# Scores of a forgetting attention: three float32r products of two-part queries and keys in place of one float32 product

## The chip, the cores and the metric

The kernel runs on one core of one Trainium2 chip. The metric is the device time of one execution in microseconds (us); a kernel is run several times and the median is given. The engines are named as the profile names them: PE is the TensorE matmul, PEld its weight load, DVE is VectorE, ACT is ScalarE, POOL is GpSimd, SP is the queue that issues the weight transfers.

## The reference

A decoder trunk of two layers over 256 tokens of width 2048, all in float32. Layer 0 has a dilated attention beside a convolution module, layer 1 has the "second mixer", a forgetting attention of 16 heads of 128 dimensions; each layer ends with a gated feed-forward part of width 5632. The change touches the scores of the second mixer alone:

```
u = h @ w_in
q, k, v, fl = jnp.split(u, [dC, 2 * dC, 3 * dC], axis=-1)
q = q.reshape(B, S, N_HEADS_C, HEAD_DIM) * (HEAD_DIM ** -0.5)
logf = jax.nn.log_sigmoid((fl + b_f).astype(F32))
...
Fc = jnp.cumsum(logf, axis=1)
...
s = jnp.einsum("bqhe,bkhe->bhqk", qi, k, preferred_element_type=F32)
s = s + (Fi[..., :, None] - Ft[..., None, :])
s = jnp.where(ti[:, None] >= pos[None, :], s, -jnp.inf)
p = jax.nn.softmax(s, axis=-1)
```

## The kernel before

Every large product is made in float32r, a rounded form of float32, with each operand split in two parts, hi (the value rounded to float32r) and lo (what is left). The normed tokens stand in `xs` as hi and lo side by side. Weights come from memory as `raw` (1 MB transfers on the SP queue), and `stream` splits each piece: ACT writes `whi` (L95), DVE writes `wlo` (L96), with four buffers of each.

`panel_b` makes 512 output columns, transposed, in four accumulators: per 128 x 128 weight tile one product of 512 columns, hi weight by both token parts (L109), and one of 256 columns, lo weight by the hi tokens (L110). `panel_a` does the same with the tokens as the stationary operand: three products of 512 columns (L122 to L124). `whole` adds the two halves of an accumulator (ACT L116, DVE L118).

The second mixer works through four groups of four heads. For each group there is a panel of queries (`qk1`, `acc_q`, 128 + 128 products), a panel of keys (`acc_k`), then the scores, then a panel of values (`acc_v`). `qk1` ends with one multiplication of all four heads by the norm factor (L527, DVE, 128 x 1024). The first group also makes the forget gates, whose cumulative sums go by small transfers into `fq` and `fk`, tiles of only 4 rows (partitions).

`softmax_t` makes the scores of four heads, called m = 0 to 3. A head has two blocks of queries: the first looks at 128 keys, the second at 256. Each block is one float32 product of q and k (L225; 128 rows, 128 or 256 columns) and, accumulated on it, one float32r product of `fq` and `fk` (L227; 4 rows, the same columns), which adds the forget bias. DVE then adds the mask and takes the maximum (L229), ACT makes the exponentials (L235), and so on. In layer 0 the same function runs without the bias, so there the float32 products stand alone (tile `s_e`; in layer 1 `s_o`).

The order on each engine is set by a scheduler when the program is built; it puts the scores of a group into the stream of the value panel's products, three heads together and the fourth some 16 products later. Each engine works in its own order and waits only for data and for free buffers.

Of the kernel before, what the change touches and what calls it, by code (L numbers as in the profile page):

```python
# [9 lines left out]
F32 = mybir.dt.float32  # L10
F32R = mybir.dt.float32r
I32 = mybir.dt.int32
AF = mybir.ActivationFunctionType
ALU = mybir.AluOpType
AX = mybir.AxisListType

P = 128
T = 256
# [23 lines left out]
def trunk(ctx, tc, a):  # L42
    nc = tc.nc
    V, S, PE, G = nc.vector, nc.scalar, nc.tensor, nc.gpsimd
# [8 lines left out]
    def misc(name):  # L53
        return pms.tile([P, 512], F32, tag="misc", name=name)
# [58 lines left out]
    def whole(out, acc, name):  # L113

        half = wk.tile([P, T], F32, tag="half", name=f"half_{name}", bufs=3)
        S.copy(half, acc[:, T:])  # L116
        out = half if out is None else out
        V.tensor_tensor(out=out, in0=acc[:, :T], in1=half, op=ALU.add)  # L118
        return out
# [17 lines left out]
    def cols(w, panel, k0=0):  # L137

        def part(c, n):
            kt = k0 // P + c  # L140
            return w[panel, kt // 4, :, kt % 4:kt % 4 + n, :]
        return part
# [31 lines left out]
    def rstd_from(parts, n, name):  # L174

        ps = misc(f"ss_{name}")
        for t in range(2):
            for i, ssq in enumerate(parts):
                PE.matmul(ps[:, t:t + 1], ssq[:, t * P:(t + 1) * P], ones[:, 0:1], start=i == 0, stop=i == len(parts) - 1)
        r = rsqrt_cols(ps[:, 0:2], 1.0 / n, name)  # L180
        return r, along_free(r, name)
# [32 lines left out]

    ROWS = ((0, 0, P), (1, P, T))

    def softmax_t(pool, qf, kf, mask, name, bias=None, act_scale=False):
        nm = wk.tile([P, 8], F32, tag="nm", name=f"nm_{name}")
        den = wk.tile([P, 8], F32, tag="den", name=f"den_{name}")
        ps = [pool.tile([P, 384], F32, tag="pt", name=f"pt_{name}{m}", bufs=8) for m in range(4)]  # L220
        for m, p in enumerate(ps):
            s = misc(f"s_{name}{m}")
            for t, c0, nk in ROWS:
                o = s[:, c0:c0 + nk]
                PE.matmul(o, qf[:, m, t * P:(t + 1) * P], kf[:, m, 0:nk], start=True, stop=bias is None)  # L225
                if bias is not None:
                    PE.matmul(o, bias[0][:, m, t * P:(t + 1) * P], bias[1][:, m, 0:nk], start=False, stop=True)  # L227
            for t, c0, nk in ROWS:
                V.tensor_tensor_reduce(out=p[:, c0:c0 + nk], in0=s[:, c0:c0 + nk], in1=mask[:, c0:c0 + nk], scale=1.0,  # L229
                                       scalar=-3.0e38, op0=ALU.add, op1=ALU.max, accum_out=nm[:, 2 * m + t:2 * m + t + 1])  # L230
        V.tensor_scalar(out=nm, in0=nm, scalar1=-1.0, scalar2=None, op0=ALU.mult)
        for m, p in enumerate(ps):
            for t, c0, nk in ROWS:
                i = 2 * m + t
                S.activation(p[:, c0:c0 + nk], p[:, c0:c0 + nk], AF.Exp, bias=nm[:, i:i + 1], accum_out=den[:, i:i + 1])  # L235
        V.reciprocal(out=den, in_=den)
        for m, p in enumerate(ps):
            for t, c0, nk in ROWS:
                w = den[:, 2 * m + t:2 * m + t + 1]
                if act_scale:  # L240
                    S.activation(p[:, c0:c0 + nk], p[:, c0:c0 + nk], AF.Copy, scale=w)
                else:
                    V.tensor_scalar(out=p[:, c0:c0 + nk], in0=p[:, c0:c0 + nk], scalar1=w, scalar2=None, op0=ALU.mult)
            tp = misc(f"tp_{name}{m}")
            for b in range(3):
                PE.transpose(tp[:, b * P:(b + 1) * P], p[:, b * P:(b + 1) * P], ident)
            S.copy(p, tp[:, :384])
        return ps
# [12 lines left out]
    with ExitStack() as ph:  # L261
        mx = ph.enter_context(tc.tile_pool(name="mx0", bufs=1))
# [139 lines left out]
        qf = [qk_panel(512 * hg, rq, f"q{hg}") for hg in range(2)]  # L402
        pts = []
        pace[0] = P_K
        for hg in range(2):
            kf = qk_panel(1024 + 512 * hg, rb, f"k{hg}")
# [102 lines left out]
    with ExitStack() as ph:  # L509
        mx = ph.enter_context(tc.tile_pool(name="mx1", bufs=1))  # L510
        w_in, w_out = a["od_w_in"], a["od_w_out"]
        mask = mx.tile([P, 384], F32, name="mask1")
        G.dma_start(out=mask, in_=a["c_mask"][:, 384:768])
        bf = mx.tile([P, 1], F32, name="bf")
        G.memset(bf[96:P, :], 0.0)
        G.dma_start(out=bf[P - NHC:P, :], in_=a["od_b_f"].rearrange("l h -> h l"))
        y2 = mx.tile([P, KT, 2, T], F32R, name="y21")
        rcol, rb = rstd_from([ssq1], D, "m1")
        rq = mx.tile([P, T], F32, name="rq")
        V.tensor_scalar(out=rq, in0=rb, scalar1=SC, scalar2=None, op0=ALU.mult)  # L520

        def qk1(c0, r, name):
            acc = panel_b(cols(w_in, c0 // 512), x2, list(range(KT)), name)
            full = mx.tile([P, 4, T], F32, tag=name[0] + "1", name=name, bufs=2)
            for m in range(4):
                whole(full[:, m, :], acc[m], f"{name}{m}")
            V.tensor_tensor(out=full, in0=full, in1=r.unsqueeze(1).broadcast_to([P, 4, T]), op=ALU.mult)  # L527
            return full

        def forget_gates():  # L530

            acc = panel_b(lambda c, n: a["od_w_f"], x2, list(range(KT)), "fl", order=(0,))
            g0 = slice(96, P)
            z = mx.tile([P, T], F32, name="z")
            e = mx.tile([P, T], F32, name="e")
            fc = mx.tile([P, T], F32, name="fc")
            whole(z, acc[0], "fl")
            V.tensor_tensor(out=z[g0, :], in0=z[g0, :], in1=rb[g0, :], op=ALU.mult)
            V.tensor_scalar(out=z[g0, :], in0=z[g0, :], scalar1=bf[g0, :], scalar2=None, op0=ALU.add)
            V.scalar_tensor_tensor(out=e[g0, :], in0=z[g0, :], scalar=-1.0, in1=z[g0, :], op0=ALU.mult, op1=ALU.min)  # L540
            S.activation(e[g0, :], e[g0, :], AF.Exp)
            S.activation(e[g0, :], e[g0, :], AF.Ln, bias=1.0)
            V.scalar_tensor_tensor(out=z[g0, :], in0=z[g0, :], scalar=0.0, in1=e[g0, :], op0=ALU.min, op1=ALU.subtract)
            V.tensor_tensor_scan(out=fc[g0, :], data0=ones[g0, 0:1].broadcast_to([32, T]), data1=z[g0, :], initial=0.0,
                                 op0=ALU.mult, op1=ALU.add)

            fhl = mx.tile([P, 4, T], F32R, name="fhl")
            fv = fhl.bitcast(F32)
            V.tensor_copy(fhl[g0, 0, :], fc[g0, :])
            V.tensor_tensor(out=fhl[g0, 1, :], in0=fc[g0, :], in1=fv[g0, 0, :], op=ALU.subtract)  # L550
            V.tensor_scalar(out=fhl[g0, 2:4, :], in0=fv[g0, 0:2, :], scalar1=-1.0, scalar2=None, op0=ALU.mult)
            return fv

        for hg in range(4):
            qf = qk1(512 * hg, rq, f"q1{hg}")
            if hg == 0:
                fv = forget_gates()
            fq = mx.tile([4, 4, T], F32R, tag="fq", name=f"fq{hg}")
            fk = mx.tile([4, 4, T], F32R, tag="fk", name=f"fk{hg}")
            G.memset(fq.bitcast(F32), 1.0)  # L560
            G.memset(fk.bitcast(F32), 1.0)
            f0 = P - NHC + 4 * hg
            for r in range(2):
                G.dma_start(out=fq.bitcast(F32)[r:r + 1, :, :], in_=fv[f0:f0 + 4, r, :])
                G.dma_start(out=fk.bitcast(F32)[2 + r:3 + r, :, :], in_=fv[f0:f0 + 4, 2 + r, :])
            kf = qk1(2048 + 512 * hg, rb, f"k1{hg}")
            pts = softmax_t(mx, qf, kf, mask, f"o{hg}", bias=(fq, fk))
            va = panel_a(cols(w_in, 8 + hg), x2, list(range(KT)), f"v1{hg}")
            vt = mx.tile([P, 2, 512], F32, tag="vt1", name=f"vt1{hg}")
            for t in range(2):  # L570
                S.activation(vt[:, t, :], va[t], AF.Copy, scale=rcol[:, t:t + 1])
            for m in range(4):
                weigh_v(pts[m], vt, m, y2, 4 * hg + m, f"o{hg}{m}")

        ssq2 = new_ssq("f1")
        for i in range(4):
            acc = panel_b(cols(w_out, i), lambda k: y2[:, k, :, :], list(range(KT)), f"oc{i}")
            add_x(acc, i, then=lambda kt: finish_x(kt, 48 + kt, ssq2, "f1"))
# [3 lines left out]
    o = fin.tile([P, 2, D], F32, name="o")  # L582
# [141 lines left out]
```

## Time and profile before

| | us |
|---|---|
| median of 3 runs | 2268.2 |
| lowest and highest of them | 2265.68, 2268.28 |
| the profiled execution's own time | 2266.76 |
| its span, first to last instruction | 2265.0 |
| PE busy | 2226.5 (98%) |
| DVE busy | 1510.7 (67%) |
| ACT busy | 1131.3 (50%) |

The second mixer lies at about 1117 to 1510 us of the span. In the profile a matmul's duration runs from its issue to its modelled end and includes the passage through the array, so neighbours overlap: what a product costs is read from the distance to the next one's start. The records mark all matmul operands as f32, whether float32 or float32r. One float32 product written in the code stands in the trace as two weight loads and two matmuls.

### The profile page before, as it was taken

Reading aid. Unit: us, or ns where it says so; the run is one execution under the profiler, and the core shown is the slowest. Engines: PE = TensorE matmul, PEld = TensorE weight load, DVE = VectorE, ACT = ScalarE, POOL = GpSimd, SP = SyncE. Lnnn points to the kernel's source line nnn. Section 1 sums busy time; section 2 is a strip of 40 time slices with the busy share of each in tenths; the row PEclk is TensorE's granted clock in tenths of the full one; section 3 lists DMA queues with packets and bytes.
Section 4 is the critical chain, followed back from the end, with each engine's and each line's share of the span. In section 5 each row is a group of like instructions: output and inputs, shape, how many; then the busy total and the mean of one; then the engine's idle time right before and its main releaser. Section 6 shows DMA issues by size and latency. Waiting matters only on the chain.

```text
span 2265.0 us, 30815 instructions
## 1 busy us (share of the span) xinstructions
PE 2226.5 (98%) x12142; PEld 1915.6 (85%) x12142; DVE 1510.7 (67%) x2307; ACT 1131.3 (50%) x1619; POOL 45.5 (2%) x77
## 2 busy tenths in 40 slices
PE   8999889999999999999999999999999999999997
PEld 7888778888888888888888888888888888888886
DVE  6999988776754576666655555666766644676644
ACT  6667655454443344444554444555444433444433
POOL 2000000000000000000010000000000000000001
PEclk9999899999999999999999999999999999999999
DMA  7554345555555545555545444555455555545453
GB/s 254 186 183 171 129 151 186 186 186 187 186 186 194 189 176 204 185 187 186 190 151 186 166 152 165 186 186 203 177 191 192 187 187 194 193 172 203 168 190 126
DMA packets 60225, 411.90 MB, mean 182 GB/s; under 512 B 7232, under 2 KB 7936, under 8 KB 11696
## 3 DMA queue, kind: packets, MB, share of 16 engines
q1 hardware_dynamic: 59328, 408.62, 50.7%
q8 instruction: 95, 1.56, 0.3%
q10 hardware_dynamic: 144, 1.05, 0.1%
q14 instruction: 50, 0.41, 0.1%
q0 software_dynamic: 608, 0.26, 0.0%
HBM read 407.75 MB, written 2.10 MB: 181 GB/s over the span
## 4 chain that ended last, share of the span: by engine, by line
PE 97%; DVE 1%; ACT 1%; DMA 0%; issue 0%; SPq 0%; ACTq 0%; DVEq 0%
PE acc_g L109 15%; PE acc_u L109 14%; PE acc_g L110 7%; PE acc_u L110 7%; PE acc_d L109 7%; PE acc_q L109 4%; PE acc_k L109 4%; PE acc_d L110 4%; PE acc_oc L109 3%; PE acc_ag L109 2%; PE acc_q L110 2%; PE acc_k L110 2%; PE acc_v L122 2%; PE acc_v L123 2%; PE acc_d L122 2%; PE acc_d L124 2%
## 5 line engine op out<-in xcount | busy, mean ns | idle before, releaser
L109 PE MATMUL acc_g<-xs,whi_g 128*128 128x512 f32 x1408 | 493.1, 397 | 0.0
L109 PE MATMUL acc_u<-xs,whi_u 128*128 128x512 f32 x1408 | 481.9, 395 | 0.0
L110 PE MATMUL acc_g<-xs,wlo_g 128*128 128x256 f32 x1408 | 388.8, 280 | 0.0
L110 PE MATMUL acc_u<-xs,wlo_u 128*128 128x256 f32 x1408 | 370.0, 279 | 0.0
L96 DVE TENSOR_TENSOR wlo_g<-raw_g,whi_g 128x1024 fp32r<-128x1024 f32 x176 | 215.1, 1223 | 166.2 <-ACT whi_g L95 166.2
L109 PEld LDWEIGHTS acc_g<-xs,whi_g 128*128 128x128 f32 x1408 | 262.6, 188 | 60.7
L95 ACT CAST whi_u<-raw_u 128x1024 fp32r<-128x1024 f32 x176 | 185.1, 1052 | 239.9 <-PE acc_u L109 122.0
L109 PEld LDWEIGHTS acc_u<-xs,whi_u 128*128 128x128 f32 x1408 | 260.1, 188 | 52.7
L96 DVE TENSOR_TENSOR wlo_u<-raw_u,whi_u 128x1024 fp32r<-128x1024 f32 x176 | 213.1, 1221 | 116.6 <-ACT whi_u L95 116.6
L95 ACT CAST whi_g<-raw_g 128x1024 fp32r<-128x1024 f32 x176 | 184.9, 1051 | 198.1 <-PE acc_u L109 91.3
L96 DVE TENSOR_TENSOR wlo_d<-raw_d,whi_d 128x1024 fp32r<-128x1024 f32 x136 | 166.5, 1224 | 161.5 <-ACT whi_d L95 161.3
L110 PEld LDWEIGHTS acc_u<-xs,wlo_u 128*128 128x128 f32 x1408 | 265.0, 188 | 9.0
L110 PEld LDWEIGHTS acc_g<-xs,wlo_g 128*128 128x128 f32 x1408 | 265.6, 189 | 3.0 <-DVE wlo_g L96 0.2
L95 ACT CAST whi_d<-raw_d 128x1024 fp32r<-128x1024 f32 x136 | 143.0, 1051 | 207.2 <-PE acc_d L109 118.9
L109 PE MATMUL acc_d<-hp,whi_d 128*128 128x512 f32 x704 | 245.2, 394 | 0.0
L110 PE MATMUL acc_d<-hp,wlo_d 128*128 128x256 f32 x704 | 194.4, 283 | 0.0
L109 PEld LDWEIGHTS acc_d<-hp,whi_d 128*128 128x128 f32 x704 | 131.3, 188 | 28.8
L110 PEld LDWEIGHTS acc_d<-hp,wlo_d 128*128 128x128 f32 x704 | 132.3, 188 | 1.9
L109 PE MATMUL acc_q<-xs,whi_q 128*128 128x512 f32 x384 | 133.8, 396 | 0.0
L109 PE MATMUL acc_k<-xs,whi_k 128*128 128x512 f32 x384 | 131.7, 394 | 0.0
L110 PE MATMUL acc_q<-xs,wlo_q 128*128 128x256 f32 x384 | 104.5, 282 | 0.0
L110 PE MATMUL acc_k<-xs,wlo_k 128*128 128x256 f32 x384 | 102.0, 279 | 0.0
(296 smaller groups left out, 3858.4 us busy)
## 6 DMA issues: line engine op xcount, KB each, us to landing
raw_g<-in_ffn_w_up SPq DMA_DIRECT2D x88, 1024.0 KB, 4.8
raw_u<-in_ffn_w_up SPq DMA_DIRECT2D x88, 1024.0 KB, 4.8
raw_d<-in_ffn_w_down SPq DMA_DIRECT2D x68, 1024.0 KB, 4.8
raw_q<-in_od_w_in SPq DMA_DIRECT2D x16, 1024.0 KB, 4.8
raw_k<-in_od_w_in SPq DMA_DIRECT2D x16, 1024.0 KB, 4.8
raw_v<-in_od_w_in SPq DMA_DIRECT2D x16, 1024.0 KB, 4.8
raw_oc<-in_od_w_out SPq DMA_DIRECT2D x16, 1024.0 KB, 4.8
raw_e<-in_ffn_w_down SPq DMA_DIRECT2D x16, 1024.0 KB, 4.7
```

The source lines that it names most:

```text
L95: S.copy(hi, rv[:, h:h + half, :])
L96: last = V.tensor_tensor(out=lo, in0=rv[:, h:h + half, :], in1=hi.bitcast(F32), op=ALU.subtract)
L109: PE.matmul(acc[m], hi[:, j, ms], x.rearrange("p a t -> p (a t)"), start=k == 0, stop=False)
L110: PE.matmul(acc[m][:, :T], lo[:, j, ms], x[:, 0, :], start=False, stop=k == len(kts) - 1)
L122: PE.matmul(o, xh, hi, start=first, stop=False)
L123: PE.matmul(o, xh, lo, start=False, stop=False)
L124: PE.matmul(o, xl, hi, start=False, stop=last)
```

## The change

`qk1` no longer hands out the float32 queries and keys: a new function `split4` makes a hi part (ACT, a copy to float32r) and a lo part (DVE, a subtraction), each 128 x 1024, into tiles `sq` and `sk`. Each float32 product of a score becomes three float32r products of the same size: hi by hi, hi by lo, lo by hi. The bias product stays as the last of the group. The tile `full` now has one buffer shared by queries and keys; `sq` and `sk` have one each. Layer 0 keeps its float32 products.

```
+    def split4(pool, full, tag, name):
+
+        two = pool.tile([P, 2, 4, T], F32R, tag=tag, name=name, bufs=1)
+        S.copy(two[:, 0], full)
+        V.tensor_tensor(out=two[:, 1], in0=full, in1=two.bitcast(F32)[:, 0], op=ALU.subtract)
+        return two
...
-                o = s[:, c0:c0 + nk]
-                PE.matmul(o, qf[:, m, t * P:(t + 1) * P], kf[:, m, 0:nk], start=True, stop=bias is None)
-                if bias is not None:
-                    PE.matmul(o, bias[0][:, m, t * P:(t + 1) * P], bias[1][:, m, 0:nk], start=False, stop=True)
+                o, ts = s[:, c0:c0 + nk], slice(t * P, (t + 1) * P)
+                if bias is None:
+                    PE.matmul(o, qf[:, m, ts], kf[:, m, 0:nk], start=True, stop=True)
+                else:
+                    PE.matmul(o, qf[:, 0, m, ts], kf[:, 0, m, 0:nk], start=True, stop=False)
+                    PE.matmul(o, qf[:, 0, m, ts], kf[:, 1, m, 0:nk], start=False, stop=False)
+                    PE.matmul(o, qf[:, 1, m, ts], kf[:, 0, m, 0:nk], start=False, stop=False)
+                    PE.matmul(o, bias[0][:, m, ts], bias[1][:, m, 0:nk], start=False, stop=True)
...
-            full = mx.tile([P, 4, T], F32, tag=name[0] + "1", name=name, bufs=2)
+            full = mx.tile([P, 4, T], F32, tag="qk1", name=name, bufs=1)
...
-            return full
+            return split4(mx, full, name[0] + "2", f"s{name}")
```

On PE, in the value panel of the first head group, the scores stood like this (s_o00 and s_o01 are the scores of heads m = 0 and 1, acc_v10 a value accumulator; the first 128x128 and 128x256 of a head are its two blocks):

```order
L122 MATMUL acc_v10_0_10475<-whi_v10_6_10529,xs_78 128x512
L225 MATMUL s_o00_10409<-k10_10389,q10_10135 128x128
L227 MATMUL s_o00_10409<-fk0_10210,fq0_10209 128x128
L225 MATMUL s_o00_10409<-k10_10389,q10_10135 128x256
L227 MATMUL s_o00_10409<-fk0_10210,fq0_10209 128x256
L225 MATMUL s_o01_10416<-k10_10389,q10_10135 128x128
L227 MATMUL s_o01_10416<-fk0_10210,fq0_10209 128x128
```

Now the same place reads:

```order
L124 MATMUL acc_v10_0_10497<-whi_v10_6_10551,xs_78 128x512
L235 MATMUL s_o00_10415<-sk10_10406,sq10_10149 128x128
L235 MATMUL s_o01_10426<-sk10_10406,sq10_10149 128x128
L235 MATMUL s_o02_10437<-sk10_10406,sq10_10149 128x128
L122 MATMUL acc_v10_1_10498<-whi_v10_6_10551,xs_78 128x512
L123 MATMUL acc_v10_1_10498<-wlo_v10_6_10552,xs_78 128x512
L124 MATMUL acc_v10_1_10498<-whi_v10_6_10551,xs_78 128x512
L236 MATMUL s_o00_10415<-sk10_10406,sq10_10149 128x128
L237 MATMUL s_o00_10415<-sk10_10406,sq10_10149 128x128
L238 MATMUL s_o00_10415<-fk0_10213,fq0_10212 128x128
L235 MATMUL s_o00_10415<-sk10_10406,sq10_10149 128x256
L236 MATMUL s_o00_10415<-sk10_10406,sq10_10149 128x256
```

The scores begin five value products later, the first hi-by-hi products of three heads stand ahead of the rest, and every bias product still stands alone between products of 128 rows. The other three groups and the fourth head of each group change in the same way.

On ACT and DVE one instruction each is added per panel of queries and per panel of keys. On DVE, behind the key panel of the first group, before:

```order
L118 TENSOR_TENSOR k_10389<-acc_k_3_10220,half_k_10399 128x256
L527 TENSOR_TENSOR k_10389<-k_10389,rb_m_9959 128x1024
L96 TENSOR_TENSOR wlo_v_8_10548<-raw_v_8_10545,whi_v_8_10547 128x1024
L96 TENSOR_TENSOR wlo_v_10_10564<-raw_v_8_10545,whi_v_10_10563 128x1024
L229 ISA pt_o_10405,nm_o_10403<-s_o_10409,mask_9935 128x128
```

and now:

```order
L118 TENSOR_TENSOR k_10392<-acc_k_3_10220,half_k_10402 128x256
L538 TENSOR_TENSOR k_10392<-k_10392,rb_m_9959 128x1024
L221 TENSOR_TENSOR sk_10406<-k_10392,sk_10406 128x1024
L96 TENSOR_TENSOR wlo_v_8_10570<-raw_v_8_10567,whi_v_8_10569 128x1024
L96 TENSOR_TENSOR wlo_v_10_10586<-raw_v_8_10567,whi_v_10_10585 128x1024
L96 TENSOR_TENSOR wlo_v_12_10604<-raw_v_12_10601,whi_v_12_10603 128x1024
L240 ISA pt_o_10411,nm_o_10409<-s_o_10415,mask_9935 128x128
```

The split of the keys stands ahead of the next weight split (`wlo_v_8`), and the split `wlo_v_12` has moved ahead of the first maximum. On ACT the copy `sk<-k` stands ahead of `whi_v_8` in the same way, behind the last `half_k`. Nothing else moves on any engine, and POOL and SP issue what they did, in the same order.

## Rows read from the trace of the kernel before

**Rows 1.** The page's first part: busy us, share and instructions per engine.
```profile
PE 2226.5 (98%) x12142; PEld 1915.6 (85%) x12142; DVE 1510.7 (67%) x2307; ACT 1131.3 (50%) x1619; POOL 45.5 (2%) x77
```

**Rows 2.** Windows of the second mixer: busy us per engine, PE clock.
```profile
1160.00:1180.00 20.00, 20.00 (x85) 15.05 (x84) 10.17 (x25) 5.95 (x6) 2.62 (x4) 1.00 0.42 152
```

**Rows 3.** Timeline of PE, scores of the first group: start us, duration us, instruction.
```profile
1166.12 0.39 PE L122 MATMUL acc_v<-whi_v,xs 128*128 128x512 f32 x1
1166.35 0.38 PE L225 MATMUL s_o<-k,q 128*128 128x128 f32 x2
1166.66 0.32 PE L227 MATMUL s_o<-fk,fq 4*128 4x128 f32 x1
...
1167.86 0.49 PE L225 MATMUL s_o<-k,q 128*128 128x128 f32 x2
1168.27 0.32 PE L227 MATMUL s_o<-fk,fq 4*128 4x128 f32 x1
1168.53 0.70 PE L225 MATMUL s_o<-k,q 128*128 128x256 f32 x2
1169.16 0.38 PE L227 MATMUL s_o<-fk,fq 4*128 4x256 f32 x1
1169.47 0.49 PE L225 MATMUL s_o<-k,q 128*128 128x128 f32 x2
...
1170.77 0.38 PE L227 MATMUL s_o<-fk,fq 4*128 4x256 f32 x1
1171.08 0.50 PE L123 MATMUL acc_v<-wlo_v,xs 128*128 128x512 f32 x1
1171.41 0.40 PE L124 MATMUL acc_v<-whi_v,xs 128*128 128x512 f32 x1
```

**Rows 4.** Timeline of the weight loads (PEld) in the same place.
```profile
1167.85 0.30 PEld L225 LDWEIGHTS s_o<-k,q 128*128 128x128 f32 x2
...
1171.07 0.19 PEld L123 LDWEIGHTS acc_v<-wlo_v,xs 128*128 128x128 f32 x1
1171.18 0.19 PEld L124 LDWEIGHTS acc_v<-whi_v,xs 128*128 128x128 f32 x1
```

**Rows 5.** Instructions on the tile s_o: count, duration ns min/median/max.
```profile
L225 PEld LDWEIGHTS s_o<-k,q x64: 186/188/189, 1166.1 to 1406.5; 128*128 128x128 f32 x64
...
L227 PE MATMUL s_o<-fk,fq x32: 322/350/383, 1166.7 to 1407.0; 4*128 4x128 f32 x16, 4*128 4x256 f32 x16
```

**Rows 6.** Timeline of PE in layer 0: scores of three heads without bias.
```profile
197.68 0.40 PE L122 MATMUL acc_v<-whi_v,xs 128*128 128x512 f32 x1
197.91 2.13 PE L225 MATMUL s_e<-k,q 128*128 128x128 f32 x12
199.69 0.59 PE L123 MATMUL acc_v<-wlo_v,xs 128*128 128x512 f32 x1
```

**Rows 7.** Timeline of PE: a key panel's pair, and nine 128-column transposes.
```profile
1149.61 0.39 PE L109 MATMUL acc_k<-xs,whi_k 128*128 128x512 f32 x1
1149.85 0.27 PE L110 MATMUL acc_k<-xs,wlo_k 128*128 128x256 f32 x1
1149.96 0.40 PE L109 MATMUL acc_k<-xs,whi_k 128*128 128x512 f32 x1
...
1187.49 1.14 PE L246 MATMUL tp_o<-cst,pt_o 128*128 128x128 f32 x9
```

**Rows 8.** Timeline of ACT and DVE behind the key panel, first group.
```profile
1158.97 0.36 ACT L116 COPY half_k<-acc_k 128x256 f32<-128x256 f32 x1
1163.60 1.05 ACT L95 CAST whi_v<-raw_v 128x1024 fp32r<-128x1024 f32 x1 [4.27 <-PE acc_v L124]
...
1160.69 1.23 DVE L527 TENSOR_TENSOR k<-k,rb_m 128x1024 f32<-128x1024 f32 x1
1164.69 2.58 DVE L96 TENSOR_TENSOR wlo_v<-raw_v,whi_v 128x1024 fp32r<-128x1024 f32 x2 [2.77 <-ACT whi_v L95]
```

**Rows 9.** Timeline of ACT and DVE behind the query panel, second group.
```profile
1217.57 1.05 ACT L95 CAST whi_k<-raw_k 128x1024 fp32r<-128x1024 f32 x1 [3.78 <-PE acc_k L109]
...
1215.16 1.23 DVE L527 TENSOR_TENSOR q<-q,rq 128x1024 f32<-128x1024 f32 x1
1218.66 1.22 DVE L96 TENSOR_TENSOR wlo_k<-raw_k,whi_k 128x1024 fp32r<-128x1024 f32 x1 [2.28 <-ACT whi_k L95]
```

## Prediction

> **What bounds the kernel now.** I read the shares of the page first: PE is busy 98% of the span, DVE 67%, ACT 50% [rows 1]. Then the windows of the second mixer: PE is busy in all of each of them, at a granted clock of 1.00, the 2.4 GHz level, while ACT and DVE have idle time [rows 2]. So PE's stream of products is the bound in the place that the change touches. A microsecond saved there is a microsecond of the span, and work added to ACT or DVE costs nothing unless it makes a product late.
>
> Then the timeline of PE, to price a score. From start to start, a middle head takes: float32 block of 128 columns 0.41 us (1167.86 to 1168.27), its bias product 0.26, float32 block of 256 columns 0.63, its bias product 0.31; 1.61 us a head [rows 3], some 25.8 us for the 16 heads. The counts agree: 64 float32 records, 32 bias records [rows 5].
>
> These four numbers show what a score really pays for. The two bias products differ by 0.05 us for 128 columns, which is one column per cycle at 2.4 GHz (0.053). So the columns of a bias product take 0.05 and 0.11 us, and 0.20 remains in both. The two float32 blocks differ by 0.22 for 128 columns: four cycles a column. Their columns take 0.21 and 0.43, and again 0.20 remains. Every change between a product of 128 rows and one of 4 rows thus costs 0.20 us on top of the columns, four times a head: 0.8 of the 1.61 us. Part of it is seen in the loads: behind a bias product the weight load starts together with its own product (1167.85 and 1167.86, 1171.07 and 1171.08), where in the stream it starts one product earlier; the next load follows 0.11 later [rows 3, 4]. So 0.11 is an uncovered load and 0.09 is the rest.
>
> Is it the 4 rows or the change from float32r to float32? Layer 0 tells. There float32 scores stand between float32r products with no bias. The last float32 product ends at 197.91 + 2.13 = 200.04, the next float32r one at 199.69 + 0.59 = 200.28: 0.24 later, which is a 512-column product's normal step (1149.61 to 1149.85) [rows 6, 7]. Behind the bias product of layer 1 the same step from end to end is 0.43 (1170.77 + 0.38 = 1171.15 to 1171.08 + 0.50 = 1171.58), although both are float32r [rows 3]. So the number of rows makes the cost, not the type.
>
> **The change part by part.** *Bias products.* They stay, each alone between products of 128 rows, in the new order too. Four changes of 0.20 a head remain: nothing saved.
>
> *Blocks of 256 columns.* Three float32r products in place of four cycles a column. A float32r product of 256 columns takes 0.11 to 0.12 in a stream (1149.85 to 1149.96; the whole pair 0.35, of it 0.23 to 0.24 for the 512 columns) [rows 7]. Three make 0.11 + 0.12 + 0.12 = 0.35, in place of 0.43: 0.08 saved a head.
>
> *Blocks of 128 columns.* No float32r product of 128 columns and 128 rows is in the trace. Its columns need 0.05, as those of the bias product. But each brings a load of 128 x 128, and loads follow each other at 0.11 (1171.07, 1171.18) [rows 4]; a chain of nine 128-column transposes, each with its load, also moves at (1.14 - 0.27) / 8 = 0.11 with 0.27 for one transpose [rows 7]. So the second and third product go by the load: 0.05 + 0.11 + 0.11 = 0.27 in place of 0.21, 0.06 more a head. Where the first product of three heads stands ahead among the value products, it pays its 0.11 there; the sum is the same. Before, a float32 block hid its second load under 0.11 of columns, which is why it was not dearer.
>
> Bounds for this unknown step: 0.05, if loads hid completely; 0.19, if each load took its whole duration by itself (186 to 189 ns) [rows 5]. I take 0.11, the row nearest in shape. With 0.05 throughout (and 0.107 for 256 columns, 0.32 for three) a head saves 0.05 + 0.11 = 0.16, or 2.6 us over 16 heads. With 0.19 it loses 0.22 - 0.08 = 0.14, or 2.2 us.
>
> The Trainium skill speaks of the loads: "TensorE: Matmul & The Clock Gate", section "Weight-path perf modes — Fast Weight Load (FWL) and DoubleRow", has weights load several times faster when there are 128 of them and the type is not FP32. If float32r counted as such a type, the products would go by columns alone, and the sum by that page is the low bound, an estimate of 2.6 us saved. The trace speaks against it: float32r loads last 0.19 us, as long as the float32 ones [rows 4, 5].
>
> *The splits.* Eight copies on ACT at 1.05 and eight subtractions on DVE at 1.23 (the durations of the weight splits of the same size), 8.4 and 9.8 us. Behind the first key panel the multiplication ends at 1161.92; the copy then runs to about 1163.0 and the subtraction to 1164.3. The next cast on ACT had waited until 1163.60 for a buffer that PE frees, the next split on DVE until 1164.69 [rows 8]: both fit into idle time. The scores stood at 1166.35 and now come about 1.1 later, so hi has some 4 us in hand and lo over 3. Behind a query panel it is tightest: multiplication to 1216.39, copy to 1217.45 against a cast at 1217.57, subtraction to 1218.7 against 1218.66 [rows 9]. The 0.05 that DVE may slip is covered by the four weight buffers, which ACT fills only as PE frees them. If this cover were gone, the whole 2.3 us would show at each of eight splits. The single buffers of `full`, `sq` and `sk` are freed by work that lies a panel earlier: no wait.
>
> *Behind the scores.* The fourth head keeps its place, and the maximum, the exponentials and the transposes follow at the same distance; the weight split moved ahead of the first maximum runs before that score is ready.
>
> **Sum.** 16 x (0.06 - 0.08) = -0.3 us: 2266.5 for the profiled execution's 2266.76, and 2267.9 against the median, which is 1.4 above that execution. What is said to be removed, a float32 product, was half a switching cost that stays, and a fourth pass saved is paid back in weight loads.
>
> **The rivals.** A measurement of this kernel tells a change of about 0.2%, 4.5 us, from none.
>
> *The switch gets cheaper* (faster). If the change from 128 rows to the bias product cost 0.20 only behind a float32 product, 32 of the 64 changes would go: 32 x 0.20 = 6.4 us more, 2261.5. For it: only that order is in the trace. Against it: the way back from the bias product costs the same between two float32r products [rows 3], and float32 against float32r costs nothing in layer 0 [rows 6]. 8%. That all 64 went (12.8 us, 2255) is excluded by the way back; 1%.
>
> *The short product is slow* (slower). A float32r product of 128 columns with all rows might take four cycles a column, as float32 does: 0.21 each. The three would cost 0.64 in place of 0.21, a head 0.43 - 0.08 = 0.35 more, the 16 heads 5.6 us: 2273.8. It decides from 0.19 a product on (0.57 for three, 4.5 us in all). Against it: the bias product, float32r with 128 columns, is 0.05 shorter than the one with 256, where it would be 0.10 longer [rows 3]. 4%.
>
> *Loads don't overlap* (slower). Each float32r product of a group might wait for its own uncovered load of 0.11. Then 128 columns cost 0.05 + 2 x 0.16 = 0.37 (0.16 more) and 256 columns 0.11 + 2 x 0.22 = 0.55 (0.12 more): 4.5 us, 2272.7. Against it: in the key panel load and product overlap [rows 7]. 2%. The Trainium skill, same page, section "The mechanism", has loads overlap a running product only where the row groups differ, which would make this rival the rule; the pair of the key panel, all of it on 128 rows, disagrees.
>
> **How the numbers follow.** My forecast, no measurable change, has 85%. Its own range is 2265.6 to 2270.4 by the bounds of the 128-column step; the runs of before scatter by 2.6 us, so I widen it by about 1 at the low end, where also the rivals weigh more, and take 2264.5 to 2270.5. It leaves out all the rivals (15%) and little else. Faster 0.09, same 0.85, slower 0.06.
>
> **What would show it.** Right: PE records up by 32; no wait of PE on `sq` or `sk`; the 128-column group 0.47 from its first product to the bias (with 0.20), the 256-column group 0.55; the bias products still 0.26 and 0.31; a middle head 1.55 to 1.63. Wrong: bias products that start 0.2 sooner, loads less than 0.11 apart, 128-column products 0.19 or more apart, or a PE wait in the value panels.

## The result, and the profile after

The changed kernel takes 2273.2 us (median of 8 runs, 2271.95 to 2275.87) against 2267.86 of the kernel before (8 runs, 2265.68 to 2269.16): 1.0024 times as long, 95% interval 1.0015 to 1.0033. It is slower by 5.3 us; I had forecast no change, and the time lies outside my range.

The first part of the page after, which answers to [rows 1], looks as forecast: 32 more records on PE, 8 more on DVE and on ACT, the same shares.

```profile
PE 2233.7 (98%) x12174; PEld 1926.3 (85%) x12174; DVE 1521.0 (67%) x2315; ACT 1139.6 (50%) x1627; POOL 46.1 (2%) x77
```

The time is lost inside the second mixer. From the first product of the forget gates (`acc_fl`) to the first of the output projection (`acc_oc`) it was 1416.3 - 1130.2 = 286.1 us, by the instruction lists of the two tiles:

```profile
L109 PE MATMUL acc_fl<-xs,whi_fl x16: 392/394/395, 1130.2 to 1135.4; 128*128 128x512 f32 x16
...
L109 PE MATMUL acc_oc<-y,whi_oc x256: 388/394/484, 1416.3 to 1509.6; 128*128 128x512 f32 x128
```

And after:

```profile
L109 PE MATMUL acc_fl<-xs,whi_fl x16: 391/394/396, 1131.2 to 1136.4; 128*128 128x512 f32 x16
...
L109 PE MATMUL acc_oc<-y,whi_oc x256: 389/394/485, 1423.3 to 1516.6; 128*128 128x512 f32 x128
```

That is 292.1, 6.0 more. The list of PE's waits has none in this part. The timeline of PE at the scores of the first group, the place of [rows 3], shows what happened (start us, duration us, instruction):

```profile
1168.49 0.45 PE L235 MATMUL s_o<-sk,sq 128*128 128x128 f32 x3
1168.78 0.45 PE L122 MATMUL acc_v<-whi_v,xs 128*128 128x512 f32 x1
...
1170.91 0.33 PE L236 MATMUL s_o<-sk,sq 128*128 128x128 f32 x1
1171.07 0.28 PE L237 MATMUL s_o<-sk,sq 128*128 128x128 f32 x1
1171.28 0.32 PE L238 MATMUL s_o<-fk,fq 4*128 4x128 f32 x1
1171.53 0.39 PE L235 MATMUL s_o<-sk,sq 128*128 128x256 f32 x1
1171.76 0.28 PE L236 MATMUL s_o<-sk,sq 128*128 128x256 f32 x1
1171.87 0.28 PE L237 MATMUL s_o<-sk,sq 128*128 128x256 f32 x1
1172.08 0.38 PE L238 MATMUL s_o<-fk,fq 4*128 4x256 f32 x1
1172.39 0.33 PE L236 MATMUL s_o<-sk,sq 128*128 128x128 f32 x1
...
1174.06 0.58 PE L238 MATMUL s_o<-fk,fq 4*128 4x256 f32 x1
1174.57 0.80 PE L122 MATMUL acc_v<-whi_v,xs 128*128 128x512 f32 x1
1175.16 0.63 PE L123 MATMUL acc_v<-wlo_v,xs 128*128 128x512 f32 x1
1175.59 0.63 PE L124 MATMUL acc_v<-whi_v,xs 128*128 128x512 f32 x1
```

The second head goes as worked out: 1.48 us (1170.91 to 1172.39), and its first product, drawn ahead, 0.1 more (three of them from 1168.49 to 1168.78), some 1.58 where a float32 head took 1.61. The bias products are unchanged at 0.25 and 0.31, the three products of 256 columns go at 0.23, 0.11 and 0.21 with the change of rows behind them. But in the third head everything stretches, and the value products behind it step by 0.43 us (1175.16 to 1175.59) in place of 0.23. That is about half speed. The windows of three such places (busy us per engine, then PE's granted clock):

```profile
1172.80:1179.50 6.70, 6.70 (x18) 5.08 (x18) 2.21 (x7) 1.04 (x1) 0.00 (x0) 0.50 0.00 0
1329.80:1333.10 3.30, 3.30 (x10) 2.40 (x9) 0.64 (x4) 0.80 (x1) 0.00 (x0) 0.51 0.00 0
1408.40:1411.70 3.30, 3.30 (x9) 2.53 (x9) 1.04 (x5) 1.04 (x1) 0.00 (x0) 0.50 0.00 0
```

The granted clock is at its lower level, 1.2 GHz, for 6.7 + 3.3 + 3.3 = 13.3 us, each time from the end of a three-head stretch of scores on, or from its third head on in the first group. In the kernel before it is 1.00 over the whole part, as in [rows 2]:

```profile
1130.00:1416.00 286.00, 286.00 (x1494) 239.81 (x1493) 156.39 (x254) 136.06 (x221) 13.42 (x22) 1.00 0.46 163
```

The second group of the changed kernel kept its clock, so it shows what the products themselves save. Its value panel, with the scores in it, lasts from the first product on `acc_v` to the first on `acc_q` of the next group. Before:

```profile
1234.60 0.39 PE L122 MATMUL acc_v<-whi_v,xs 128*128 128x512 f32 x1
...
1262.87 0.39 PE L109 MATMUL acc_q<-xs,whi_q 128*128 128x512 f32 x1
```

And after:

```profile
1238.65 0.39 PE L122 MATMUL acc_v<-whi_v,xs 128*128 128x512 f32 x1
...
1266.90 0.39 PE L109 MATMUL acc_q<-xs,whi_q 128*128 128x512 f32 x1
```

It takes 28.25 us in place of 28.27: 0.1 us saved over four groups. The groups with a fall take 31.30, 29.76 and 29.79 us, 6.1 more in all. So the falls cost 6.1 us, the products saved 0.1, and the part grew by 6.0. PE counts as busy in all of these windows: the column of busy time does not tell.

Behind the first key panel, as in [rows 8], the split is where I had put it and delays nothing (ACT, then DVE):

```profile
1162.96 1.05 ACT L220 CAST sk<-k 128x1024 fp32r<-128x1024 f32 x1 [2.62 <-DVE k L538]
1164.61 1.06 ACT L95 CAST whi_v<-raw_v 128x1024 fp32r<-128x1024 f32 x1 [0.60 <-PE acc_v L124]
...
1164.05 1.23 DVE L221 TENSOR_TENSOR sk<-k,sk 128x1024 fp32r<-128x1024 f32 x1 [1.12 <-ACT sk L220]
1165.70 3.95 DVE L96 TENSOR_TENSOR wlo_v<-raw_v,whi_v 128x1024 fp32r<-128x1024 f32 x3 [0.43 <-ACT whi_v L95]
```

The cast of the weights still waits for PE, not for the split.

### The profile page after: what moved, and what is told of

Read it like the earlier page. It is cut to its first block, busy times and chain, and to the rows that moved or that the text cites. A ratio compares the mean times of both kernels' runs of the same rounds, so it can differ in the third digit from the quotient of the medians.

```text
span 2272.0 us, 30894 instructions
## 1 busy us (share of the span) xinstructions
PE 2233.7 (98%) x12174; PEld 1926.3 (85%) x12174; DVE 1521.0 (67%) x2315; ACT 1139.6 (50%) x1627; POOL 46.1 (2%) x77
## 4 chain that ended last, share of the span: by engine, by line
PE 96%; DVE 2%; ACT 1%; DMA 0%; issue 0%; SPq 0%; ACTq 0%; DVEq 0%
PE acc_g L109 14%; PE acc_u L109 14%; PE acc_g L110 7%; PE acc_u L110 7%; PE acc_d L109 7%; PE acc_k L109 4%; PE acc_q L109 4%; PE acc_d L110 4%; PE acc_oc L109 3%; PE acc_ag L109 2%; PE acc_v L122 2%; PE acc_q L110 2%; PE acc_v L123 2%; PE acc_v L124 2%; PE acc_k L110 2%; PE acc_d L122 2%
```

## The experiments

Theory A: the clock falls because the three-head stretch of scores streams too little through the array. A head's columns in that stretch took 0.21 + 0.05 + 0.43 + 0.11 = 0.80 of 1.61 us before; in the changed kernel they take 0.05 + 0.05 for the two products left of the first block, 0.05 for its bias, 3 x 0.11 and 0.11 for the second block, 0.59 of 1.48. Most of the rest of the time goes to changes of the row count, 0.20 each. Theory B: the splits or the shift in time do it. Theory C, formed after the first runs: float32r scores do it, whatever their columns.

Unless another fence is shown, falls of the clock are read from windows of 25 us around the scores of the four groups in the profiled execution of each kernel: a window at 0.93 has one short fall.

**The splits alone.** To the kernel before:

```
+            split4(mx, full, "qk2", f"s{name}")
             return full
```

The function is that of the change, and `full` has one buffer in place of two here too.

> The kernel before with the eight splits of queries and keys added on ACT and DVE; the scores stay float32 products of the unsplit tiles and nobody reads the parts. Theory A (the clock falls because the three-head stretch of float32r scores streams fewer columns per microsecond than the float32 one): no fall of the clock between 1150 and 1430 us, 2267 to 2269. Theory B (the added work on ACT and DVE, or the shift in time that it brings, is what costs): falls there as in the changed kernel, or PE waits, 2271 or more.

2268.75 us, ratio 1.0002 (0.9993 to 1.0011). The clock is 1.00 around all four groups, and from `acc_fl` to `acc_oc` it is 286.1 us, as before. The splits cost nothing here; theory B falls.

**Heads apart, with float32r and with float32 scores.** In both kernels one head's scores are given between two pieces of the value panel:

```
-            pts = softmax_t(mx, qf, kf, mask, f"o{hg}", bias=(fq, fk))
-            va = panel_a(cols(w_in, 8 + hg), x2, list(range(KT)), f"v1{hg}")
+            pts = softmax_t(mx, qf, kf, mask, f"o{hg}", bias=(fq, fk), apart=True)
+            pts, head, finish = pts
+
+            def between(i):
+                if i in (3, 4, 5, 6):
+                    head((3, 4, 5, 6).index(i))
+                if i == (3, 4, 5, 6)[3]:
+                    finish()
+
+            va = panel_a(cols(w_in, 8 + hg), x2, list(range(KT)), f"v1{hg}", between)
...
```

> The changed kernel with the same products, but the four heads of a group stand apart in the value panel, twelve value products between two heads. Theory A: no fall of the clock in the second mixer, 2266.5 to 2269. Theory B, or a cost that lies in the float32r products wherever they stand: 2272 to 2275.

> The kernel before with float32 scores, the four heads of a group apart in the value panel as in spread_after. Theory A: no fall of the clock in the second mixer, as before. If the 1.2 us that spread_after showed in its key panels at full clock belong to the spreading, they show here as well and the time is 2269 to 2271; if they belong to the float32r scores, 2267 to 2268.5.

float32r apart: 2270.78, ratio 1.0012 (1.0003 to 1.0021). float32 apart: 2270.51, 1.0008 (0.9999 to 1.0018). The clock of both is 1.00 around all four groups:

```profile
1165.00:1190.00 25.00, 25.00 (x119) 20.16 (x118) 10.95 (x25) 10.84 (x19) 3.77 (x6) 1.00 0.38 130
```

(The float32r kernel, first group.) So the same number of the same float32r products meets no fall here when value products stand between the heads, and float32r and float32 take the same time, which is my sum. Both are some 2.5 us above the kernel before, more than theory A had said. The mixer accounts for 1.8 us of it in the float32r kernel (1131.0 to 1418.9) and 1.6 in the other (1131.8 to 1419.5), at full clock, so that part belongs to the spreading and not to the type of the scores. It does not lie in the value panels (28.32 and 28.26 us) but in the panels of queries and keys of the later groups: a key panel takes 22.6 us in place of 22.2. Why was not tried.

**One product in place of three.** 

```
-  PE.matmul(o, qf[:, 0, m, ts], kf[:, 1, m, 0:nk], start=False, stop=False)
-  PE.matmul(o, qf[:, 1, m, ts], kf[:, 0, m, 0:nk], start=False, stop=False)
```

> The changed kernel without the hi-by-lo and lo-by-hi products: each block is one float32r product and its bias product. At full clock this takes 0.11 + 0.11 and 0.12 + 0.12 us a head off, 7.2 us in all. Theory A: the array streams still less in the score stretches, so the clock falls there in at least three of the four groups and the time is near 2273.2 - 7.2 = 2266. If the stretch has become too short to matter, no fall there and 2260 to 2261. Theory B says nothing of it beyond 2266.

This leaves the lo parts out of the scores. 2264.06, ratio 0.9986 (0.9977 to 0.9994): between the two numbers. One fall in the profiled execution, at the second group (0.93; the others 1.00). The time between does not count the falls: here too a later key panel takes 22.6 us in place of 22.2, and a query panel 26.5 in place of 26.2, 2 us in all that the expectation did not have. The stream is thinner than in the changed kernel, but the three heads are through in 3.3 us in place of 4.3 or more. Theory A's "at least three of four" was wrong. That how long the thin stretch lasts counts too would explain it; no run changes the length alone.

**Bias tiles of 128 rows.** In the changed kernel and in the kernel before:

```
+        fq = mx.tile([P, 4, T], F32R, name="fq")
+        fk = mx.tile([P, 4, T], F32R, name="fk")
+        for f in (fq, fk):
+            G.memset(f.bitcast(F32), 0.0)
+            G.memset(f.bitcast(F32)[0:4, :, :], 1.0)
+
         for hg in range(4):
...
-            fq = mx.tile([4, 4, T], F32R, tag="fq", name=f"fq{hg}")
-            fk = mx.tile([4, 4, T], F32R, tag="fk", name=f"fk{hg}")
-            G.memset(fq.bitcast(F32), 1.0)
-            G.memset(fk.bitcast(F32), 1.0)
```

> The changed kernel with fq and fk as tiles of 128 rows, 124 of them zero, so that no product of 4 rows is left. If the number of rows makes the 0.20 us at each change, a head's blocks cost 4 x 0.11 and 4 x 0.12, 0.92 us in place of 1.58: 10.6 us less. Theory A: the array streams most of the time, so no fall of the clock: 2267.6 - 10.6 = 2257. If the clock falls with float32r scores whatever their density: 2262. If the 0.20 us has nothing to do with the rows: 2273.

> The kernel before (float32 scores) with the bias tiles of 128 rows as in wide_after, so that no product changes the number of rows. A head's blocks then cost 0.21 + 0.11 + 0.43 + 0.11 = 0.86 us or a little less in place of 1.61: 12 us less, 2256. Against wide_after (2256.8) this says what the float32r products are worth where the changes of rows are gone: by the step of loads 0.92 to 0.86, so float32 is the same or up to 1 us faster. No fall of the clock.

float32r: 2256.82, ratio 0.9953 (0.9941 to 0.9966). float32: 2255.67, 0.9941 (0.9929 to 0.9954). Both are as expected within 0.4 us, both beat the two kernels of this study, and the clock is 1.00 around all four groups of both. A head of the float32r one on PE's timeline:

```profile
1171.81 0.22 PE L236 MATMUL s_o<-sk,sq 128*128 128x128 f32 x1
1171.87 0.28 PE L237 MATMUL s_o<-sk,sq 128*128 128x128 f32 x1
1171.99 0.27 PE L238 MATMUL s_o<-fk,fq 128*128 128x128 f32 x1
1172.10 0.33 PE L235 MATMUL s_o<-sk,sq 128*128 128x256 f32 x1
1172.27 0.28 PE L236 MATMUL s_o<-sk,sq 128*128 128x256 f32 x1
1172.38 0.28 PE L237 MATMUL s_o<-sk,sq 128*128 128x256 f32 x1
1172.50 0.28 PE L238 MATMUL s_o<-fk,fq 128*128 128x256 f32 x1
1172.62 0.22 PE L236 MATMUL s_o<-sk,sq 128*128 128x128 f32 x1
```

The seven products take 0.81 us a head, 0.12 each on the mean (single steps are 0.06 to 0.17; their loads start 0.11 to 0.12 apart), and about 0.9 with the product drawn ahead. The bias product, 32 times its rows, steps by 0.11 and 0.12 where it cost 0.25 and 0.31. So the number of rows did make the 0.20 us, and the step of 0.11 for 128 columns, which I had only bounded, is right. The float32 head takes 0.89 (1166.63 to 1167.52): three float32r products are worth no more than one float32 product here.

**More columns.** Three kernels add work to the changed one. The first widens the three products of each first block to 256 columns:

```
+  full = s[:, c0:c0 + T]
-  PE.matmul(o, qf[:, 0, m, ts], kf[:, 0, m, 0:nk], start=True, stop=False)
+  PE.matmul(full, qf[:, 0, m, ts], kf[:, 0, m, :], start=True, stop=False)
...
```

> The changed kernel with the three float32r products of each first block made 256 columns wide; the 128 columns too many are overwritten by the second block, so the scores are the same. This is added work: three products take 0.35 in place of 0.27 us, 0.08 a head, 1.3 us in all. Theory A (the clock falls because the score stretch streams too few columns per microsecond): columns rise from 0.64 to 0.80 us a head, as much as in the float32 kernel, so no fall in the second mixer and about 2267.5. Theory C (the clock falls with float32r scores between changes of row count, whatever the columns): falls stay and 2274.5. In between if some falls stay.

2274.85, ratio 1.0025 (1.0016 to 1.0033): the number of theory C. The profiled execution, 2270.91, has a single fall (fourth group, 0.93). I had counted columns that are not in the stretch: the first products of three heads are drawn ahead of it, so it streamed 0.69 of 1.55 us, not 0.80. The next two change the order so that nothing is drawn ahead, the second of them with all products of a first block 256 columns wide:

```
-  PE.matmul(o, qf[:, 0, m, ts], kf[:, 0, m, 0:nk], start=True, stop=False)
-  PE.matmul(o, qf[:, 0, m, ts], kf[:, 1, m, 0:nk], start=False, stop=False)
+  PE.matmul(o, qf[:, 0, m, ts], kf[:, 1, m, 0:nk], start=True, stop=False)
   PE.matmul(o, qf[:, 1, m, ts], kf[:, 0, m, 0:nk], start=False, stop=False)
+  PE.matmul(o, qf[:, 0, m, ts], kf[:, 0, m, 0:nk], start=False, stop=False)
```

> The changed kernel with the three products of a block in the order hi by lo, lo by hi, hi by hi. They all wait for the lo part, so none is drawn ahead, and each head's whole score stands in the three-head stretch: 0.64 us of columns in 1.59 us a head, 40%, as in the changed kernel's stretch (0.59 in 1.49). Theory A (the clock falls because the stretch between two runs of value products streams few columns): falls as in the changed kernel, 2271 to 2275. If the order of the products made it fall: no falls, 2268.

> As lo_first, and all four products of each first block are 256 columns wide (the columns too many are overwritten by the second block, the scores are the same). Added work of 0.08 + 0.05 us a head, 2.1 us in all; the stretch now streams 0.85 us of columns in 1.72 us a head, 50%, the share of the float32 kernel; in dense_after it was 0.69 in 1.55, 45%, because the products drawn ahead stood outside. Theory A: no falls in the second mixer, 2268.1 - 0.3 + 2.1 = 2270. Theory C (float32r scores make the clock fall whatever their columns): falls as before, 2273.2 + 2.1 = 2275.

The order alone: 2273.88, 1.0026 (1.0017 to 1.0036), falls at all four groups:

```profile
1165.00:1190.00 25.00, 25.00 (x110) 19.89 (x109) 12.32 (x33) 12.78 (x26) 3.80 (x6) 0.93 0.28 104
1240.00:1265.00 25.00, 25.00 (x109) 19.95 (x108) 12.54 (x29) 10.57 (x23) 3.81 (x6) 0.93 0.37 127
1318.00:1343.00 25.00, 25.00 (x109) 19.91 (x108) 12.54 (x29) 10.36 (x23) 3.80 (x6) 0.93 0.36 127
1396.00:1421.00 25.00, 25.00 (x108) 19.94 (x107) 12.42 (x27) 10.04 (x23) 0.00 (x0) 0.93 0.35 126
```

Widened: 2274.9, 1.0026 (1.0017 to 1.0035). Its profiled execution, 2270.31, has one fall, at the second group; the others lie up to 2277.17, with mean clocks of 0.989 to 0.992. In the profiled execution the falls became rarer but did not go, although the columns took the same share of the stretch as in the float32 kernel. On the share of columns alone theory A fails here.

**The two that decide.** What is left is theory C, or a theory A in which a column of 4 rows counts for less than a full one. One kernel makes float32 scores thin without any float32r product of queries and keys:

```
+                    bm = (o, bias[0][:, m, t * P:(t + 1) * P], bias[1][:, m, 0:nk])
+                    PE.matmul(*bm, start=False, stop=False)
+                    PE.matmul(o[:, 0:32], bias[2], bias[2][:, 0:32], start=False, stop=False)
+                    PE.matmul(*bm, start=False, stop=True)
...
```

`bm` is the bias product with half of its value, `bias[2]` a float32r tile of zeros with 128 rows.

> The kernel before, float32 scores, with each bias product given as two halves (the same operands with 0.5 in place of 1) and a product of zeros, 128 rows by 32 columns, between them; the scores are the same. That adds two more changes of the row count to each block: 0.46 and 0.53 us, 0.99 a head, 15.9 us, so 2284 at full clock. No float32r score is in it; in a stretch of some 7.8 us the array streams 0.64 us of full-row columns in 2.60 us a head, 25%. Theory A (a thinner stream makes the clock fall, whatever the type): falls behind every group's stretch, 2290 to 2300. Theory C (it takes float32r scores): no falls in the second mixer, 2284.

2301.11, ratio 1.0146 (1.0132 to 1.0159). The clock falls at every group; windows of the four score stretches and what follows them:

```profile
1165.00:1190.00 25.00, 25.00 (x87) 17.84 (x86) 8.28 (x22) 9.45 (x22) 3.79 (x6) 0.80 0.25 89
1250.00:1275.00 25.00, 25.00 (x86) 17.89 (x86) 8.30 (x22) 8.11 (x21) 3.80 (x6) 0.80 0.25 89
1335.00:1360.00 25.00, 25.00 (x86) 18.07 (x86) 8.31 (x22) 8.14 (x21) 3.79 (x6) 0.80 0.24 88
1420.00:1445.00 25.00, 25.00 (x86) 18.13 (x85) 8.29 (x22) 8.10 (x21) 0.00 (x0) 0.80 0.24 87
```

0.80 over 25 us is 10 us at half clock. At the rate of the changed kernel (3.05 us lost in the 6.7 us of its first group) that is some 4.6 us a group and 18 in all, an estimate; 15.9 more by the added changes of rows makes 34, and 33 was measured. Theory C is refuted as it was put: no float32r product of queries and keys is needed. Two things changed besides the columns: the zeros are themselves a float32r product on 128 rows, and the stretch of three heads is longer (7.8 us at full clock by the expectation, 4.7 before). The other adds a fourth product, lo by lo, to the widened kernel:

```
+  PE.matmul(full, qf[:, 1, m, ts], kf[:, 1, m, :], start=False, stop=False)
```

> As dense_lo_first with the fourth product, lo by lo, added to each block, 256 columns like the others: added work of 0.12 us a block, 3.8 us in all, and a stretch that streams 1.07 us of columns in 1.96 us a head, 54% (0.85 us of them with all rows, 44%; in the float32 kernel 0.64 in 1.61, 40%; in dense_lo_first 0.64 in 1.72, 37%). Theory A, with the 4-row products counting little: no falls in the second mixer, 2270 + 3.8 = 2274. Theory C: falls as in dense_lo_first or more, 2278 or above.

2272.97, ratio 1.0024 (1.0015 to 1.0033), in the windows no fall at any group:

```profile
1165.00:1190.00 25.00, 25.00 (x119) 19.95 (x118) 13.20 (x34) 13.40 (x26) 3.79 (x6) 1.00 0.33 114
1240.00:1265.00 25.00, 25.00 (x117) 19.92 (x116) 12.28 (x25) 10.45 (x22) 3.80 (x6) 1.00 0.37 127
1318.00:1343.00 25.00, 25.00 (x118) 19.89 (x117) 12.24 (x26) 10.34 (x22) 3.79 (x6) 1.00 0.37 127
1396.00:1421.00 25.00, 25.00 (x117) 19.92 (x116) 12.24 (x26) 10.39 (x22) 0.00 (x0) 1.00 0.36 126
```

It does 32 products more than the widened kernel, 3.8 us of added work by the expectation, and its time is no higher: the intervals of the two overlap. Its mean clocks are 0.991 to 0.994, those of the widened one 0.989 to 0.992.

The kernel with the new order alone, the widened one and the one with four products are the cleanest comparison: none draws a product ahead, the changes of the row count are the same, and columns are added to each block. By their medians they stand 5.9, 6.9 and 5.0 us above the kernel before. Of this the added work is 0, 2.1 and 5.6 us, by value panels without a fall (28.77 us widened, 29.65 with four products, against 28.25). That leaves 5.9 and 4.8 us for falls, and nothing with four products. With four products the stretch of three heads is the longest of the three, 5.7 us against 4.7 and 5.1, so it isn't the length that takes the falls away. Single executions with four products still go up to 2277.47, and no trace shows where they lose it.

**A thin float32 stretch by leaving work out.**

```
+        ROWS = ((0, 0, P), (1, P, T)) if bias is None else ((0, 0, P), (1, T, P))
...
```

It leaves out the first 128 keys of every second block, so it does not compute the reference.

> The kernel before, float32 scores, with the second block of queries looking at 128 keys only (its first 128 keys are left out, and their weights are set to zero), so that both blocks have 128 columns: 0.53 us of columns in 1.34 us a head, 39%, without any float32r score. At full clock the scores are 0.05 + 0.22 shorter a head, 4.3 us: 2263.8. Theory A: falls of the clock behind these stretches, 2265.5 to 2270. Theory C: no falls in the second mixer, 2263.8 or, with less work behind it, no lower than 2262.

2265.74, ratio 0.999 (0.9981 to 0.9999). The profiled execution, 2263.07, has no fall in the mixer, which is theory C's number; others of its runs went up to 2271.33 with mean clocks down to 0.990. Its value panels there take 27.22 us in place of 28.27, 4.2 less in all, but the median is only 2.2 below the kernel before. Where the other executions lost the rest no trace shows, so this one stays undecided.

## Why the prediction was wrong

*The products: right.* A float32r head at 1.58 against 1.61, three float32r products of 256 columns cheaper, three of 128 columns dearer by the pace of the loads, 0.11. My sum of -0.3 us met -0.1 at full clock, by the value panel of the group that kept its clock (28.25 against 28.27), and the two kernels with heads apart agree (28.32 and 28.26).

*The bias products: right.* The four changes of rows a head stayed, 0.20 each. That they, and not float32, are the dear part is shown by the bias tiles of 128 rows: 11 to 12 us for the 16 heads, against nothing for the change studied.

*The splits: right.* They lie in idle time; alone they change the time by a factor of 1.0002.

*The rivals.* None of mine came true. The slow short product (2273.8) and the loads that don't overlap (2272.7) gave nearly the measured time and are both refuted by the timeline: 128-column products step by 0.11, and the loads overlap. That their numbers came so near is luck. No rival of mine named the clock.

*What failed* is the step at the very start: "PE is busy in all of each of them, at a granted clock of 1.00". I read it as a property of the place and priced every product at 2.4 GHz, before and after. It was a property of the stream. The change removes columns and nearly leaves the time (0.59 of 1.48 us a head in the stretch, 0.80 of 1.61 before), and in three of four groups the clock fell to 1.2 GHz from the end of the stretch on and took the value products with it: 6.1 us lost, 0.1 saved, 6.0 in the mixer. The other 1.0 us by which the profiled spans differ (2272.0 to 2265.0) lies ahead of it, 1131.2 against 1130.2, where the change touches nothing. There the clock falls too, before and after, and not alike in every execution: between 244 and 324 us it was 0.89 on the mean before and 0.87 after.

What is shown, for the profiled executions: the falls come with the uninterrupted three-head stretch (apart, none), come with float32 scores too when their stretch is made thinner and longer, and are gone when enough products are added to the stretch with its changes of row count left as they are. With bias tiles of 128 rows there are none either, but there the stretch is also denser and only 2.4 and 2.7 us long, so that the changes of row count are needed is not shown by itself. The Trainium skill says in "TensorE: Matmul & The Clock Gate", section "What's actually happening", that the clock is granted by how busy PE has been. The falls here stand where PE shows as busy throughout, so they do not agree with it if busy is read from that column of the profile. The Trainium skill says in "Trainium Kernel Development and Optimization", section "Performance Expectations", that matmul busy time is a bad measure of how close a kernel is to its roofline, since matmuls are pipelined. I had read PE's 98% as a full engine.

What stays open: why the widened kernel, with the float32 kernel's share of columns, still lost its clock in some executions, while the thin float32 kernel, with the share of the changed one, kept it in the profiled execution. That 4-row columns count for less fits the widened kernel and the one with four products, but it was not measured by itself. Nor can I say what a group's place in time adds: of four equal groups one kept its clock in the changed kernel, and executions of the same widened kernel lie between 2270.31 and 2277.17.

## What to carry to other kernels

Where PE is the bound, work out what a change does to the stream through the array, not only to its time: here fewer columns in the same time came with a lower clock for what stands behind. A cheap operation between expensive ones is priced by what it breaks: here a 4-row product cost 0.20 us at each side, and filling it up with zeros to 128 rows gave 11 to 12 us where trading float32 for float32r gave nothing. For a block of small products, taking the changes of row count out gained most here (2256.82 with 128 rows); putting dense products between its pieces kept the clock too, but cost time of its own (2270.78).

## What the runs showed that I had not expected

The granted clock fell while PE had no idle time in the records. A kernel with 32 more products (2272.97) was no slower than the one without them (2274.9); its mean clocks were 0.991 to 0.994 against 0.989 to 0.992. A product on 128 rows, 124 of them zero, is cheaper than one on 4 rows among products of 128: 0.11 against 0.25 us for 128 columns. And three float32r products cost a float32 product's time: at 128 columns they go no faster than the loads, 0.11 us each. A fall of the clock cost 1.5 us for 3.3 us at the lower level.
